# Three small edits in a fused encoder layer: the order of the halves in the w2 tails, the engine of softplus's small steps, and the place of one preparation call

## The chip, the cores and the metric

The kernel runs on one core of one Trainium2 chip, as a single program. The metric is the device time of that program in microseconds: the median of three runs before the change is 1110.12 us (1110.07 to 1110.47). The matrix engine is called PE, the vector engine DVE, the activation engine ACT, GpSimd POOL, and the queue that issues most loads SP.

## The reference, cut to what matters

One layer of a streaming encoder on 512 tokens of width 1024, all in float32:

```python
f = swiglu(rms_norm(h, ffn1_pre_g), w1, w3, w2)       # (silu(u @ w1) * (u @ w3)) @ w2, hidden width 2816
h = h + 0.5 * rms_norm(f, ffn1_post_g)
u = rms_norm(h, mix_pre_g)
q, k, v, xr, xg = split(u @ w_in)
...                                                    # rg_lru uses softplus(-lambda), 1024 values
h = h + rms_norm(merged @ w_o, mix_post_g)
f = swiglu(rms_norm(h, ffn2_pre_g), w1, w3, w2)
y = h + 0.5 * rms_norm(f, ffn2_post_g)
```

The part between is a gated linear recurrence and a windowed attention. Of it only `softplus(-lambda)` matters here: it is computed once for 1024 channels, laid out as 128 partitions by 8 columns, and its results `chalf` and `cneg` are read by the recurrence first at 395.8 us, some 85 us after they are written.

## The kernel before

**Numbers in pairs.** Every float32 operand of a product is split into a high part `hi` (ACT copies it to the matrix engine's rounded float32) and a low part `lo` (DVE subtracts `hi` from the operand). A product is three matmuls: hi times hi, lo times hi, hi times lo. So each weight tile of 128x1024 costs one ACT copy of about 1.05 us and one DVE subtraction of about 1.14 us.

**Order.** The order of instructions on each engine is the order in which the program calls them; every engine runs its own list in that order and waits for what it needs. There is no planner. Buffers in SBUF come from 42 slots of one size, handed out in rotation.

**FFN, up.** `Pairs` (from line 689) computes two columns of blocks of `w1` or `w3` at a time by a seven-product block scheme, with sums and differences of blocks. FFN 1 runs 18 such jobs. While a job's products run on PE, `prep` prepares the next job's operands. In the last job the calls `ahead` and `tail` (both mean `half.prep(half.ready + 1)`) prepare the operands of the first units of the following stage instead.

**FFN, down.** `w2` is handled in two parts. `Halves.run` does rows 4 to 19 of 22 by the same kind of block scheme over halves of 512 columns, in 28 units of 12 matmuls each (lines 616 to 618). `Halves.prep` prepares a unit five units ahead: an ACT copy and a DVE subtraction of the weights, the same for the activations, and one or two DVE sums of blocks (lines 548 and 551). Hooks at given units start other work; one of them, at unit 25 (`SOFTPLUS_AT`), is `softplus`.

The other six rows of `w2` (`TAIL`) follow in `tok_gemm`: for each of the four token tiles t (128 tokens each), PE does 18 matmuls for columns 0 to 511 (n = 0) and 18 for columns 512 to 1023 (n = 1), lines 242 to 244. For t = 0 and 1 both column halves have a part of the block result in SBUF that has to be added (`hc`, from `Halves.part`). For t = 2 and 3 only n = 1 has such a part; n = 0 is complete in PSUM.

**The norm behind the tail.** `post_norm` (line 284) takes a tile's two halves: DVE adds the SBUF parts (line 294), ACT squares and sums each half (line 298), DVE multiplies by the gain `gpost` (line 299, `fg`), a reciprocal root follows (lines 256 to 264), and DVE adds the result to `h` (line 310). In FFN 1 `norms` (line 314) goes on with the next norm (gain `gpre`, `mix_pre_g`) and gives `hg` (lines 325, 333, 334), which PE transposes (line 343, `tr`) after the next tile's matmuls. In FFN 2 the result goes to the output.

The two gains are broadcast to all partitions by DMAs that POOL issues (`bcast`, line 281), called right after the last `w2` row is split; POOL then scales `gpre` (line 410). POOL's earlier work there is DMAs with accumulation (lines 588, 594, 602). While the tail runs, DVE also splits the first four tiles of `xr` (line 179), the first weights of the mixing stage.

`softplus` (line 1121) is two ACT steps and 29 DVE steps on 128x8 or smaller tiles: a chain of a reciprocal and a polynomial (lines 1126 to 1136), the two results, and five copies of biases times 0.5 (lines 1139 and 1143).

Of the kernel before, what the change touches and what calls it, by code (L numbers as in the profile page):

```python
# [12 lines left out]
AF = mybir.ActivationFunctionType  # L13
ALU = mybir.AluOpType
# [3 lines left out]
D = 1024  # L18
# [3 lines left out]
NT = SEQ // P  # L22
# [4 lines left out]
EPS = 1e-6  # L27
# [4 lines left out]
V_CW, V_CB, V_BA, V_BX, V_LAM, V_BG, V_G1, V_SINK, V_N = 0, 32, 40, 48, 56, 64, 80, 88, 104  # L32
# [19 lines left out]
def hybrid_layer(ctx: ExitStack, tc: tile.TileContext, a: dict, out: bass.AP):  # L52
    nc = tc.nc
    act, dve, pool, pe, sp = nc.scalar, nc.vector, nc.gpsimd, nc.tensor, nc.sync
# [38 lines left out]
    h = {}  # L93
# [142 lines left out]
    def mm_tok(acc, x, t, w, first, last, ns=(0, 1), skip=False):  # L236

        wh, wl = w
        c = slice(t * P, (t + 1) * P)
        for n in ns:  # L240
            s = slice(n * 512, (n + 1) * 512)
            pe.matmul(acc[n], x[:, 0, c], wh[:, s], start=first, stop=False, skip_group_check=skip)  # L242
            pe.matmul(acc[n], x[:, 0, c], wl[:, s], start=False, stop=False, skip_group_check=skip)  # L243
            pe.matmul(acc[n], x[:, 1, c], wh[:, s], start=False, stop=last, skip_group_check=skip)  # L244
# [3 lines left out]
    NEWT = -0.5 * D**0.5  # L248
# [32 lines left out]
        pool.dma_start(out=t, in_=bass.AP(tensor=src.tensor, offset=src.offset, ap=[[0, P], [1, D]]))  # L281
        return t

    def post_norm(acc, t, gpost, scale, dst, after=None, last=False, eps=D * EPS, mid=None, part=None):

        ss = small(2, "ss")
        fg = slot([P, D], name="fg")
        junk = slot([P, D], name="junk")
        cs = [slice(n * 512, (n + 1) * 512) for n in range(2)]
        if part:  # L290
            acc = list(acc)
            for n, o in enumerate(part):
                if o is not None:
                    dve.tensor_tensor(out=o, in0=acc[n], in1=o, op=ALU.add)
                    acc[n] = o
        rs = Rstd2()
        for n, c in enumerate(cs):
            act.activation(junk[:, c], acc[n], AF.Square, accum_out=ss[:, n : n + 1])
            dve.scalar_tensor_tensor(out=fg[:, c], in0=acc[n], scalar=scale, in1=gpost[:, c], op0=ALU.mult, op1=ALU.mult)
            if n:  # L300
                rs.root(ss)
            else:
                rs.first(ss, eps)
        r = rs.value()
        if mid:
            mid()
        if last:
            cs = [slice(0, 512), slice(512, 768), slice(768, D)]
        for n, c in enumerate(cs):
            dve.scalar_tensor_tensor(out=dst[:, c], in0=fg[:, c], scalar=r, in1=h[t][:, c], op0=ALU.mult, op1=ALU.add)  # L310
            if after:
                after(n, c)

    def norms(acc, t, gpost, scale, gpre, spill, eps, mid=None, part=None):

        hg = slot([P, D], name="hg")
        junk = slot([P, D], name="junk")
        ss = small(2, "ss")
        rs = Rstd2()

        def half(n, c):
            act.activation(junk[:, c], h[t][:, c], AF.Square, accum_out=ss[:, n : n + 1])
            if n:
                rs.first(ss)
                dve.tensor_tensor(out=hg[:, c], in0=h[t][:, c], in1=gpre[:, c], op=ALU.mult)

        post_norm(acc, t, gpost, scale * NEWT, h[t], half, eps=eps, mid=mid, part=part)
# [5 lines left out]
        dve.scalar_tensor_tensor(out=hg[:, :512], in0=ht[:, :512], scalar=r, in1=gpre[:, :512], op0=ALU.mult, op1=ALU.mult)  # L333
        act.activation(hg[:, 512:], hg[:, 512:], AF.Copy, scale=r)
        return hg
# [30 lines left out]
    def tok_gemm(nm, xs, n, R, gpost_name, scale, gpre_name, first, x_to=None, xf=None, spill=False, then=None, eps=None, pre=None):  # L366
# [36 lines left out]
        tail = list(pre.hid.seq) if pre else list(range(F, n))  # L403
# [3 lines left out]
        gpost = bcast(gpost_name)  # L407
        gpre = bcast(gpre_name) if gpre_name else None
        if gpre_name:
            pool.tensor_scalar(out=gpre, in0=gpre, scalar1=NEWT, scalar2=None, op0=ALU.mult)  # L410
        us, trs = {}, {}
        ep = lambda t: D * EPS if eps is None else eps[:, t : t + 1]
        split_to(st["get"] + len(first))
        dma_to(st["split"] + 2)
        for t in range(NT):
            for ns in ((0,), (1,)):
                for k in tail:
                    new = k == tail[0] and (t > 1 and ns == (1,) if pre else k == 0)
                    mm_tok(accs(t), xs[k], t, w[k], new, k == tail[-1], ns, bool(pre))
            if not gpre_name:  # L420
                o = slot([P, D], name="o")

# [3 lines left out]
                post_norm(acc[t], t, gpost, scale * NEWT, o, store, t == NT - 1, part=pre and pre.part(t))  # L426
# [8 lines left out]
            us[t] = norms(acc[t], t, gpost, scale, gpre, spill, ep(t), part=pre and pre.part(t))  # L435
            if t == 1:
                transpose_out(trs[t - 1], t - 1, xf)
        if not gpre_name:
# [2 lines left out]
        t = NT - 1  # L441
# [16 lines left out]
        us[t] = norms(acc[t], t, gpost, scale, gpre, spill, ep(t), between, pre and pre.part(t))  # L458
# [230 lines left out]
    class Pairs:  # L689
# [65 lines left out]
        def run(self, tail, hooks={}):  # L755
# [3 lines left out]
            last = silu = lambda: None  # L759
            for n, (nm, f) in enumerate(self.jobs):  # L760
# [23 lines left out]
                if n == len(self.jobs) - 1:  # L784
                    silu()
                    silu = lambda: None
                    tail()
                self.prep(n + 1, 2)

                def c11():  # L790
                    mm_s(W["a12"], X["b21"], bc)
                    del W["a11"], W["a12"]
                    dve.tensor_tensor(out=c[:, 0, :256], in0=bc, in1=q1, op=ALU.add)
# [11 lines left out]
                dve.tensor_tensor(out=c[:, 1, 256:], in0=v, in1=q5, op=ALU.add)  # L805
                if n == len(self.jobs) - 1:
                    tail()
                    c11()
                if not first:
                    c1 = self.c1[f]  # L810
# [310 lines left out]
    def softplus():  # L1121
        lam = vec[:, V_LAM : V_LAM + KT]
        z = [small(KT, "z", 5) for _ in range(5)]
        act.activation(z[0], lam, AF.Abs)
        act.activation(z[1], z[0], AF.Exp, scale=-1.0)
        dve.tensor_scalar(out=z[2], in0=z[1], scalar1=2.0, scalar2=None, op0=ALU.add)
        dve.reciprocal(z[2], z[2])
# [6 lines left out]
        dve.tensor_tensor(out=z[3], in0=z[3], in1=z[1], op=ALU.mult)  # L1134
        dve.tensor_scalar(out=z[4], in0=lam, scalar1=-1.0, scalar2=0.0, op0=ALU.mult, op1=ALU.max)
        dve.scalar_tensor_tensor(out=z[3], in0=z[3], scalar=2.0, in1=z[4], op0=ALU.mult, op1=ALU.add)
        dve.tensor_scalar(out=chalf, in0=z[3], scalar1=2.0, scalar2=None, op0=ALU.mult)
        dve.tensor_scalar(out=cneg, in0=z[3], scalar1=-4.0, scalar2=None, op0=ALU.mult)
# [96 lines left out]
    half = None  # L1235
# [527 lines left out]
```

## Time and profile before

| | |
|---|---|
| median of three runs | 1110.12 us |
| profiled execution, its own time | 1110.68 us |
| span of its instructions | 1108.9 us |
| PE busy | 1098.4 us, 99% of the span |
| DVE busy | 912.5 us, 82% |
| ACT busy | 668.9 us, 60% |
| POOL busy | 389.9 us, 35% |
| w2 block units of FFN 1 | 232.5 to 310 us |
| w2 tail of FFN 1 with its norms | 310 to 353 us |
| last matmul of the kernel | issued at 1100.92 us |

PE is counted busy while a matmul is under way, so its 99% says that it is hardly ever without one, and that what is left to win are the short places where a matmul starts late. The other engines work beside it; their shares are averages over stages in which each of them is at some time the one that PE waits for. The profiled execution is 0.56 us above the median.

### The profile page before, as it was taken

The page shows a single profiled execution, that of the slowest core. Times are in us where ns is not written, and L with a number is a line of the kernel's source. Part 1 is how long each engine was busy: PE and PEld are TensorE (multiplying, and loading weights), DVE is VectorE, ACT ScalarE, POOL GpSimd, SP SyncE. Part 2 cuts the span into 40 slices and gives each one's busy share as a digit, 9 for nine tenths or more (in the row PEclk, how much of TensorE's full clock was granted, in tenths as well). Part 3 has the DMA queues.
Part 4 walks back from the last instruction along what each step waited for, and adds up shares of the span by engine and source line. Part 5 has one row for each costly group of instructions (what it writes and reads, how often), then busy time and mean ns, then how long its engine had stood idle before and what let it go on. Part 6 is the DMA issues. An engine that isn't in the chain of part 4 may idle for free.

```text
span 1108.9 us, 17987 instructions
## 1 busy us (share of the span) xinstructions
PE 1098.4 (99%) x6850; PEld 989.6 (89%) x6850; DVE 912.5 (82%) x1337; ACT 668.9 (60%) x1175; POOL 389.9 (35%) x308
## 2 busy tenths in 40 slices
PE   9999999999999999999999999999999999999997
PEld 8899999987879878899888888889999999998885
DVE  5988999999997978887778867767789898689954
ACT  7755555576857678656655654356455555567821
POOL 0143533202212413242656663010976665502100
PEclk9999999999999999999999999999999999999999
DMA  9325663467944642156132435442332323476832
GB/s 338 120 87 140 136 136 115 148 197 159 256 173 186 141 127 79 40 179 239 58 95 77 131 117 223 150 159 95 115 109 83 114 82 110 137 229 148 191 113 76
DMA packets 52662, 155.41 MB, mean 140 GB/s; under 512 B 5456, under 2 KB 7376, under 8 KB 52576
## 3 DMA queue, kind: packets, MB, share of 16 engines
q1 hardware_dynamic: 42256, 129.57, 34.0%
q0 software_dynamic: 10032, 24.16, 11.1%
q8 instruction: 54, 0.88, 0.3%
q10 hardware_dynamic: 288, 0.52, 0.2%
q14 instruction: 32, 0.26, 0.1%
HBM read 138.52 MB, written 13.62 MB: 137 GB/s over the span
## 4 chain that ended last, share of the span: by engine, by line
PE 86%; DVE 10%; DMA 2%; issue 1%; ACT 0%; POOL 0%; DVEq 0%; SPq 0%; POOLq 0%; ACTq 0%
PE c L683 12%; PE c L684 12%; PE c L685 12%; PE f L224 9%; PE f L225 9%; PE f L226 9%; DVE wlo L596 2%; PE acc L243 2%; PE acc L244 2%; PE acc L242 2%; DVE uT L214 1%; DVE raw_w2a L548 1%; PE hw L243 1%; PE hw L244 1%; PE hw L242 1%
## 5 line engine op out<-in xcount | busy, mean ns | idle before, releaser
L684 PE MATMUL c<-uT,wlo 128*128 128x256 f32 x516 | 146.1, 283 | 0.0
L685 PE MATMUL c<-uT,whi 128*128 128x256 f32 x516 | 146.1, 283 | 0.0
L683 PE MATMUL c<-uT,whi 128*128 128x256 f32 x516 | 146.1, 283 | 0.0
L683 PE MATMUL c<-Xh,whi 128*128 128x256 f32 x504 | 142.8, 283 | 0.0
L684 PE MATMUL c<-Xh,wlo 128*128 128x256 f32 x504 | 142.7, 283 | 0.0
L224 PE MATMUL f<-uT,whi 128*128 128x512 f32 (+1 forms) x368 | 136.5, 371 | 0.0
L225 PE MATMUL f<-uT,wlo 128*128 128x512 f32 (+1 forms) x368 | 134.9, 367 | 0.0
L226 PE MATMUL f<-uT,whi 128*128 128x512 f32 (+1 forms) x368 | 134.8, 366 | 0.0
L685 PE MATMUL c<-Xl,whi 128*128 128x256 f32 x456 | 129.1, 283 | 0.0
L214 DVE TENSOR_TENSOR wlo<-S,whi 128x1024 fp32r<-128x1024 f32 x86 | 118.7, 1380 | 8.1 <-POOL OL L1557 4.5
L213 ACT ACTIVATE whi<-S 128x1024 fp32r<-128x1024 f32 x86 | 88.5, 1054 | 31.4 <-DVE S L732 29.7
L684 PEld LDWEIGHTS c<-uT,wlo 128*128 128x128 f32 x516 | 99.1, 192 | 0.2
L683 PEld LDWEIGHTS c<-uT,whi 128*128 128x128 f32 x516 | 99.1, 192 | 0.2
L685 PEld LDWEIGHTS c<-uT,whi 128*128 128x128 f32 x516 | 99.1, 192 | 0.0
L683 PEld LDWEIGHTS c<-Xh,whi 128*128 128x128 f32 x504 | 96.8, 192 | 0.3 <-issue 0.3
L684 PEld LDWEIGHTS c<-Xh,wlo 128*128 128x128 f32 x504 | 96.8, 192 | 0.0
L685 PEld LDWEIGHTS c<-Xl,whi 128*128 128x128 f32 x456 | 87.6, 192 | 0.0
L224 PEld LDWEIGHTS f<-uT,whi 128*128 128x128 f32 x368 | 69.4, 189 | 12.5 <-issue 1.7
L226 PEld LDWEIGHTS f<-uT,whi 128*128 128x128 f32 x368 | 69.4, 188 | 11.4
L225 PEld LDWEIGHTS f<-uT,wlo 128*128 128x128 f32 x368 | 69.5, 189 | 10.8
L1505 POOL TENSOR_SCALAR P<-P,d 128x256 f32<-128x256 f32 (+1 forms) x64 | 62.0, 984 | 45.0 <-DVE d L1503 27.9
L616 PE MATMUL hw<-wlo,uT 128*128 128x512 f32 x192 | 75.2, 392 | 0.4 <-DMA wlo<-in_w2b_dram 0.3
(434 smaller groups left out, 3189.7 us busy)
## 6 DMA issues: line engine op xcount, KB each, us to landing
raw_w2a<-in_w2a_dram SPq DMA_DIRECT2D x22, 512.0 KB, 4.5
raw_w1b<-in_w1b_dram SPq DMA_DIRECT2D x22, 512.0 KB, 4.3
raw_w3b<-in_w3b_dram SPq DMA_DIRECT2D x22, 512.0 KB, 4.3
raw_w2b<-in_w2b_dram SPq DMA_DIRECT2D x22, 512.0 KB, 4.6
raw_w3a<-in_w3a_dram SPq DMA_DIRECT2D x21, 512.0 KB, 4.4
raw_w1a<-in_w1a_dram SPq DMA_DIRECT2D x20, 512.0 KB, 4.5
raw_wg<-in_wg_dram SPq DMA_DIRECT2D x16, 512.0 KB, 4.0
h<-in_x_dram SPq DMA_DIRECT2D x8, 512.0 KB, 6.9
```

The lines of the kernel that those rows point to most:

```text
L213: act.activation(hi, src, AF.Copy)
L214: dve.tensor_tensor(out=lo, in0=src, in1=f32(hi), op=ALU.subtract)
L224: pe.matmul(ps[:, c0:c1], wh[:, s], h_, start=k == 0 and c0 == 0, stop=False, skip_group_check=True)
L225: pe.matmul(ps[:, c0:c1], wl[:, s], h_, start=False, stop=False, skip_group_check=True)
L226: pe.matmul(ps[:, c0:c1], wh[:, s], l_, start=False, stop=k == KT - 1, skip_group_check=True)
L242: pe.matmul(acc[n], x[:, 0, c], wh[:, s], start=first, stop=False, skip_group_check=skip)
L243: pe.matmul(acc[n], x[:, 0, c], wl[:, s], start=False, stop=False, skip_group_check=skip)
L616: pe.matmul(ps, xs[:, 0, j, c], lo[:, j, :], start=False, stop=False, skip_group_check=True)
L683: pe.matmul(ps, wh[:, s], xh, start=first, stop=False, skip_group_check=True)
L684: pe.matmul(ps, wl[:, s], xh, start=False, stop=False, skip_group_check=True)
L685: pe.matmul(ps, wh[:, s], xl, start=False, stop=k == 3, skip_group_check=True)
L1505: pool.tensor_scalar(out=pt[:, x, b0:256], in0=pt[:, x, b0:256], scalar1=d[:, x : x + 1], scalar2=None, op0=ALU.mult)
```

## The change

Three edits.

1. For t = 2 and 3 of both w2 tails PE does n = 1 first and n = 0 second. `post_norm` now goes over the halves in the same order, and does each half whole (add, square, multiply by the gain) before it turns to the other one. For t = 0 and 1 the order of the halves stays 0, 1, but the DVE add of the second half now stands behind the first half's multiplication and its small step of line 256, where before both adds came first.
2. In `softplus`, DVE keeps three steps (add 2, reciprocal, the maximum `z[4]`). The rest, 26 DVE instructions, becomes 28 POOL instructions (two fused steps are written as two each).
3. In the last job of FFN 1's `Pairs`, the first `tail()`, which prepares unit 2 of the block units, is called after the product `s3` and its two additions rather than before the product `s4`. FFN 2's job (`self.R` is None) stays as it was.

```diff
-    def post_norm(acc, t, gpost, scale, dst, after=None, last=False, eps=D * EPS, mid=None, part=None):
+    def post_norm(acc, t, gpost, scale, dst, after=None, last=False, eps=D * EPS, mid=None, part=None, ns=(0, 1)):
...
-        if part:
-            acc = list(acc)
-            for n, o in enumerate(part):
-                if o is not None:
-                    dve.tensor_tensor(out=o, in0=acc[n], in1=o, op=ALU.add)
-                    acc[n] = o
         rs = Rstd2()
-        for n, c in enumerate(cs):
-            act.activation(junk[:, c], acc[n], AF.Square, accum_out=ss[:, n : n + 1])
-            dve.scalar_tensor_tensor(out=fg[:, c], in0=acc[n], scalar=scale, in1=gpost[:, c], op0=ALU.mult, op1=ALU.mult)
-            if n:
+        for j, n in enumerate(ns):
+            c, x, o = cs[n], acc[n], part and part[n]
+            if o is not None:
+                dve.tensor_tensor(out=o, in0=x, in1=o, op=ALU.add)
+                x = o
+            act.activation(junk[:, c], x, AF.Square, accum_out=ss[:, j : j + 1])
+            dve.scalar_tensor_tensor(out=fg[:, c], in0=x, scalar=scale, in1=gpost[:, c], op0=ALU.mult, op1=ALU.mult)
+            if j:
                 rs.root(ss)
             else:
                 rs.first(ss, eps)
...
+        halves = lambda t: (1, 0) if pre and t > 1 else (0, 1)
...
-            for ns in ((0,), (1,)):
+            for n_ in halves(t):
                 for k in tail:
-                    new = k == tail[0] and (t > 1 and ns == (1,) if pre else k == 0)
-                    mm_tok(accs(t), xs[k], t, w[k], new, k == tail[-1], ns, bool(pre))
+                    new = k == tail[0] and (t > 1 and n_ == 1 if pre else k == 0)
+                    mm_tok(accs(t), xs[k], t, w[k], new, k == tail[-1], (n_,), bool(pre))
...
                 if n == len(self.jobs) - 1:
                     silu()
                     silu = lambda: None
-                    tail()
+                    if self.R is None:
+                        tail()
                 self.prep(n + 1, 2)
...
                 if n == len(self.jobs) - 1:
                     tail()
+                    if self.R is not None:
+                        tail()
                     c11()
...
         dve.tensor_scalar(out=z[2], in0=z[1], scalar1=2.0, scalar2=None, op0=ALU.add)
         dve.reciprocal(z[2], z[2])
-        dve.tensor_tensor(out=z[1], in0=z[1], in1=z[2], op=ALU.mult)
-        dve.tensor_tensor(out=z[2], in0=z[1], in1=z[1], op=ALU.mult)
-        dve.tensor_scalar(out=z[3], in0=z[2], scalar1=1.0 / 17, scalar2=1.0 / 15, op0=ALU.mult, op1=ALU.add)
+        dve.tensor_scalar(out=z[4], in0=lam, scalar1=-1.0, scalar2=0.0, op0=ALU.mult, op1=ALU.max)
+        e = pool
+        e.tensor_tensor(out=z[1], in0=z[1], in1=z[2], op=ALU.mult)
+        e.tensor_tensor(out=z[2], in0=z[1], in1=z[1], op=ALU.mult)
+        e.tensor_scalar(out=z[3], in0=z[2], scalar1=1.0 / 17, scalar2=None, op0=ALU.mult)
+        e.tensor_scalar(out=z[3], in0=z[3], scalar1=1.0 / 15, scalar2=None, op0=ALU.add)
         for c in (13, 11, 9, 7, 5, 3, 1):
-            dve.tensor_tensor(out=z[3], in0=z[3], in1=z[2], op=ALU.mult)
-            dve.tensor_scalar(out=z[3], in0=z[3], scalar1=1.0 / c, scalar2=None, op0=ALU.add)
+            e.tensor_tensor(out=z[3], in0=z[3], in1=z[2], op=ALU.mult)
+            e.tensor_scalar(out=z[3], in0=z[3], scalar1=1.0 / c, scalar2=None, op0=ALU.add)
...
-        dve.tensor_scalar(out=bhalf, in0=vec[:, V_BA : V_BG + 16], scalar1=0.5, scalar2=None, op0=ALU.mult)
+        e.tensor_scalar(out=bhalf, in0=vec[:, V_BA : V_BG + 16], scalar1=0.5, scalar2=None, op0=ALU.mult)
...
-                dve.tensor_scalar(
+                e.tensor_scalar(
                     out=bxh[r0 : r0 + 64, par, :], in0=vec[64 * par : 64 * par + 64, V_BX : V_BX + KT],
```

More of the change, by code (lines that the diff above doesn't have):

```diff
@@ L312, in post_norm, with norms @@
                 after(n, c)
-    def norms(acc, t, gpost, scale, gpre, spill, eps, mid=None, part=None):
+    def norms(acc, t, gpost, scale, gpre, spill, eps, mid=None, part=None, ns=(0, 1)):
         hg = slot([P, D], name="hg")
@@ L325, in half @@
                 dve.tensor_tensor(out=hg[:, c], in0=h[t][:, c], in1=gpre[:, c], op=ALU.mult)
-        post_norm(acc, t, gpost, scale * NEWT, h[t], half, eps=eps, mid=mid, part=part)
+        post_norm(acc, t, gpost, scale * NEWT, h[t], half, eps=eps, mid=mid, part=part, ns=ns)
         ht = h[t]
@@ L424, in store @@
                     sp.dma_start(out=out[t * P : (t + 1) * P, c], in_=o[:, c])
-                post_norm(acc[t], t, gpost, scale * NEWT, o, store, t == NT - 1, part=pre and pre.part(t))
+                post_norm(acc[t], t, gpost, scale * NEWT, o, store, t == NT - 1, part=pre and pre.part(t), ns=halves(t))
                 continue
@@ L434, in tok_gemm @@
                 transpose_out(trs[t - 1], t - 1)
-            us[t] = norms(acc[t], t, gpost, scale, gpre, spill, ep(t), part=pre and pre.part(t))
+            us[t] = norms(acc[t], t, gpost, scale, gpre, spill, ep(t), part=pre and pre.part(t), ns=halves(t))
             if t == 1:
@@ L457, in tok_gemm @@
         mm_feat(bs[0], ws[0], 0, 256, ks=range(3, KT))
-        us[t] = norms(acc[t], t, gpost, scale, gpre, spill, ep(t), between, pre and pre.part(t))
+        us[t] = norms(acc[t], t, gpost, scale, gpre, spill, ep(t), between, pre and pre.part(t), halves(t))
         transpose_out(trs[t - 1], t - 1, parts=(1,))
@@ L1127, in softplus @@
         dve.reciprocal(z[2], z[2])
-        dve.tensor_tensor(out=z[1], in0=z[1], in1=z[2], op=ALU.mult)
-        dve.tensor_tensor(out=z[2], in0=z[1], in1=z[1], op=ALU.mult)
-        dve.tensor_scalar(out=z[3], in0=z[2], scalar1=1.0 / 17, scalar2=1.0 / 15, op0=ALU.mult, op1=ALU.add)
-        for c in (13, 11, 9, 7, 5, 3, 1):
-            dve.tensor_tensor(out=z[3], in0=z[3], in1=z[2], op=ALU.mult)
-            dve.tensor_scalar(out=z[3], in0=z[3], scalar1=1.0 / c, scalar2=None, op0=ALU.add)
-        dve.tensor_tensor(out=z[3], in0=z[3], in1=z[1], op=ALU.mult)
@@ L1135, in softplus @@
[L1135 to L1138, printed above, removed]
-        dve.tensor_scalar(out=bhalf, in0=vec[:, V_BA : V_BG + 16], scalar1=0.5, scalar2=None, op0=ALU.mult)
+        dve.tensor_scalar(out=z[4], in0=lam, scalar1=-1.0, scalar2=0.0, op0=ALU.mult, op1=ALU.max)
@@ new lines, in softplus @@
+        e.tensor_tensor(out=z[3], in0=z[3], in1=z[1], op=ALU.mult)
+        e.tensor_scalar(out=z[3], in0=z[3], scalar1=2.0, scalar2=None, op0=ALU.mult)
+        e.tensor_tensor(out=z[3], in0=z[3], in1=z[4], op=ALU.add)
+        e.tensor_scalar(out=chalf, in0=z[3], scalar1=2.0, scalar2=None, op0=ALU.mult)
+        e.tensor_scalar(out=cneg, in0=z[3], scalar1=-4.0, scalar2=None, op0=ALU.mult)
+        e.tensor_scalar(out=bhalf, in0=vec[:, V_BA : V_BG + 16], scalar1=0.5, scalar2=None, op0=ALU.mult)
```

## The prediction

> **What bounds the kernel now.** First the page and the waits of PE, then the order of time on DVE, POOL and PE around the places that the diff touches.
>
> ```profile
> span 1108.9 us, 17987 instructions
> PE hw L243 <- DVE wlo L179: 0.7, 1, 0.7
> PE c L683 <- ACT ct L804: 0.3, 1, 0.3
> ```
>
> The waits' columns are the total in us, how often, and the longest. Of a span of 1108.9 us, the sums to win on PE are these two waits, and what lies behind the last matmul. So the change can win at most about 2 us; what it can lose is not bounded by that. The first wait is at 314 us, in the w2 tail of FFN 1. The order of time on DVE there (start, duration):
>
> ```profile
> 306.63 0.16 DVE L1126 TENSOR_SCALAR z<-z 128x8 f32<-128x8 f32 x1
> 306.82 0.20 DVE L1127 RECIPROCAL z<-z 128x8 f32<-128x8 f32 x1
> 312.84 0.69 DVE L214 TENSOR_TENSOR hT<-kept,hT 128x512 fp32r<-128x512 f32 x1
> 313.45 1.22 DVE L179 TENSOR_TENSOR wlo<-raw_w2a,whi 128x1024 fp32r<-128x1024 f32 x1
> 314.59 4.62 DVE L179 TENSOR_TENSOR wlo<-raw_xr,whi 128x1024 fp32r<-128x1024 f32 x4
> 319.13 1.28 DVE L294 TENSOR_TENSOR hc<-hw,hc 128x512 f32<-128x512 f32 x2
> 320.33 0.68 DVE L299 SCALAR_TENSOR_TENSOR fg<-hc,bc_ffn_post_g 128x512 f32<-128x512 f32 x1
> 320.93 0.20 DVE L256 TENSOR_SCALAR b<-ss,veps 128x1 f32<-128x1 f32 x1
> 325.01 0.69 DVE L325 TENSOR_TENSOR hg<-h,bc_mix_pre_g 128x512 f32<-128x512 f32 x1
> 326.50 0.75 DVE L333 SCALAR_TENSOR_TENSOR hg<-h,r,bc_mix_pre_g 128x512 f32<-128x512 f32 x1
> 333.70 0.75 DVE L333 SCALAR_TENSOR_TENSOR hg<-h,r,bc_mix_pre_g 128x512 f32<-128x512 f32 x1
> ```
>
> And on PE:
>
> ```profile
> 314.73 0.50 PE L243 MATMUL hw<-wlo,hT 128*128 128x512 f32 x1 [0.67 <-DVE wlo L179]
> 327.60 0.60 PE L343 MATMUL tr<-ident,hg 128*128 128x128 f32 x4
> 336.65 0.60 PE L343 MATMUL tr<-ident,hg 128*128 128x128 f32 x4
> ```
>
> Softplus holds DVE from 306.63 to 312.84, and the last `w2` split (313.45) stands behind it; PE waits 0.67 us for that split. The row to keep in mind is 327.60: PE transposes tile 0's `hg`, which DVE finished at 326.50 + 0.75 = 327.25. That is 0.35 us before PE wanted it. Whatever delays tile 0's norm by more than that delays PE.
>
> **Edit 2: what POOL's queue carries.** After the change softplus stands on POOL ahead of these three:
>
> ```profile
> 299.85 0.59 POOL L281 DMA_DIRECT2D bc_ffn_post_g<-in_ffn_post_g_dram  x1 [11.95 <-PE hw L617]
> 304.06 0.55 POOL L281 DMA_DIRECT2D bc_mix_pre_g<-in_mix_pre_g_dram  x1 [3.62 <-DVE wlo L596]
> 311.38 2.79 POOL L410 TENSOR_SCALAR bc_mix_pre_g<-bc_mix_pre_g 128x1024 f32<-128x1024 f32 x1 [6.77 <-DMA bc_mix_pre_g<-in_mix_pre_g_dram]
> ```
>
> These are the gains' broadcasts. `gpost` is issued at 299.85, before softplus begins, and line 299 reads it at 320.33. POOL's first small step needs DVE's reciprocal (306.82 + 0.20), so POOL starts softplus at about 307.1 and issues `gpost` only when its 28 steps are done, at a time T. The trace shows no POOL step of 8 columns. The nearest rows (duration minimum/median/maximum in ns, and one group with its idle time):
>
> ```profile
> L1505 POOL TENSOR_SCALAR P<-P,d x64: 592/922/1804, 527.8 to 654.8; 128x256 f32<-128x256 f32 x48, 128x128 f32<-128x128 f32 x16
> L1557 POOL TENSOR_TENSOR OL<-o,OH x16: 729/735/1474, 559.8 to 677.3; 128x256 fp32r<-128x256 f32 x16
> L1362 POOL TENSOR_TENSOR xf<-xf,xf x4: 2412/3262/3272, 355.9 to 365.1; 128x1024 f32<-128x1024 f32 x4
> L737 POOL TENSOR_TENSOR S<-S,raw_w1b 128x512 f32<-128x512 f32 x10 | 16.7, 1668 | 0.8
> ```
>
> Two inputs: 729 ns at 256 columns and 2412 at 1024 give 2.19 ns a column and 168 ns fixed, so 0.19 us at 8 columns. One input: 592 at 128 (the minimum) and 922 at 256 give 2.58 ns a column and 262 fixed, 0.28 us at 8; line 410's 2.79 us at 1024 leaves only about 0.15 fixed, 0.17 at 8; I take 0.23 between them. Steps that read the step before start 0.08 us later (line 737: 0.8 us over 10). So 11 x 0.19 + 17 x 0.23 + 22 x 0.08 = 7.8 us, or 0.28 us a step, if POOL is left alone: T = 314.9. From above, no step costs more than the 592 ns of the smallest one measured.
>
> POOL is not left alone. In another stage, POOL's rows and DVE's of the same moments, the last one the same line on DVE without POOL:
>
> ```profile
> 124.19 2.25 POOL L736 TENSOR_TENSOR S<-raw_w3a 128x512 f32<-128x512 f32 x1 [5.21 <-PE c L685]
> 126.53 2.16 POOL L737 TENSOR_TENSOR S<-S,raw_w3a 128x512 f32<-128x512 f32 x1
> ...
> 124.07 1.22 DVE L214 TENSOR_TENSOR wlo<-raw_w1a,whi 128x1024 fp32r<-128x1024 f32 x1 [1.17 <-ACT whi L213]
> 125.21 2.32 DVE L823 TENSOR_TENSOR cc<-cc,Rb 128x1024 f32<-128x1024 f32 x1
> ...
> 226.91 1.22 DVE L823 TENSOR_TENSOR cc<-cc,Rb 128x1024 f32<-128x1024 f32 x1
> ```
>
> POOL's step of 124.19 ends at 126.44, some 1.15 us after DVE's subtraction of 124.07 ended at 125.29; DVE's next takes 2.32 instead of 1.22 and ends at 127.53; POOL's next ends at 128.69, again 1.16 us after that. The two take turns, one instruction each, when DVE reads two SBUF tensors. Between 307.2 and about 314.4 DVE has six such instructions: the last `hT` and `w2` splits, then four splits of `xr`. Taking turns lets POOL through once for each, so with the first step and one in a gap some 8 steps are done by 314.4. Then DVE stands at line 299 and waits for `gpost` itself, and the other 20 steps run freely: 20 x 0.26 (the last five depend on nothing before them) = 5.1 us. T = 319.5.
>
> [...]
>
> How long the broadcast then takes, for the five that line 281 issues, and how full the DMA engines are (in a row of windows the last two figures are the DMA share and GB/s):
>
> ```profile
> DMA to landing us min/median/max: 4.0/5.9/7.2
> ...
> 305.00:310.00 5.00, 5.00 (x23) 4.14 (x23) 4.45 (x19) 1.58 (x2) 0.00 (x0) 1.00 1.01 404
> 320.00:325.00 5.00, 5.00 (x24) 4.14 (x23) 3.83 (x10) 3.58 (x9) 0.00 (x0) 1.00 0.01 3
> ```
>
> At 320 to 325 us the DMA engines were idle before the change, so I take 4.0, with 7.2 for the range. `gpost` lands at 323.5. The two broadcasts no longer share the full DMA engines at 305 us, so `xr` lands earlier; that shifts DVE's six turns, not their number.
>
> [...]
>
> From there: line 299 for the first half (0.6 from start to start), line 256 (0.13), and now the second half's add behind them (0.65) with a start-up of 0.1: that add ends at 325.0. Before it ended at 319.13 + 1.28 = 320.41 and `hg` at 327.25, 6.84 us later. So `hg` is ready at 331.8 and PE's transposes start at 331.9, not 327.60: **4.3 us late**. `gpre` follows `gpost` by 0.6 us and is scaled by T + 0.6 + 4.0 + 2.8 = 326.9; line 325 wants it 2.24 us before `hg` is done, at 329.6, so it is covered by 2.7 us.
>
> The 26 steps taken from DVE bring the last `w2` split forward and end PE's 0.67 us wait. PE then only waits longer at the transposes: worth nothing here, 0.7 us if `gpost` were in time. Tile 1 is next: its norm took from 327.25 to 334.45, 7.2 us, and its second add now stands behind line 256, which waits for ACT's first sum; that adds up to 0.9. PE asks for it 336.65 - 327.60 = 9.05 us after tile 0's transposes, so it stays covered, with 0.9 us left.
>
> **Edit 1.** At the end of the kernel:
>
> ```profile
> 1101.35 0.69 DVE L294 TENSOR_TENSOR hc<-acc,hc 128x512 f32<-128x512 f32 x1 [4.01 <-PE acc L244]
> ...
> 1097.27 0.60 ACT L298 ACTIVATE junk<-hw 128x512 f32<-128x512 f32 x1 [2.30 <-PE hw L244]
> 1102.07 0.63 ACT L298 ACTIVATE junk<-hc 128x512 f32<-128x512 f32 x1 [4.12 <-DVE hc L294]
> ```
>
> The last half was the one with the add: DVE at 1101.35, then ACT's square at 1102.07. Now the last half is complete in PSUM, ACT squares it at 1101.35, in 0.60 rather than 0.63 us: **0.75 us less**, all on the path, since reciprocal root, line 310 and the store follow one another. It cannot be more than the add's 0.72 + 0.03; it would be less if ACT's start from PSUM came later than DVE's. In FFN 1 tiles 2 and 3 gain the same where PE does not wait: nothing.
>
> **Edit 3.** PE, ACT and DVE around the second wait and where PE next meets DVE:
>
> ```profile
> 229.13 1.04 ACT L591 ACTIVATE whi<-raw_w2a 128x1024 fp32r<-128x1024 f32 x1
> 230.59 0.36 ACT L804 ACTIVATE ct<-c 128x256 f32<-128x256 f32 x1
> ...
> 248.95 0.68 DVE L214 TENSOR_TENSOR uT<-hEO,uT 128x512 fp32r<-128x512 f32 x1
> ...
> 249.69 0.49 PE L617 MATMUL hw<-whi,uT 128*128 128x512 f32 x1
> ```
>
> ACT drains `s3` (line 804) at 230.59 behind unit 2's copies; called later, the copies no longer stand ahead of it, and the wait of 0.3 (0.5 with the slow start behind it) goes. But at 249.69 PE starts on an operand that DVE finishes at 249.63. DVE does the same instructions in between, without idle time, in a slightly other order, so PE gets there earlier and waits longer: **0**, with 0.5 gained or 0.3 lost (a unit's operand late) for the range. The moved call also carries one load on SP; nothing else is issued on SP between its two places.
>
> **Sum.** 4.3 - 0.75 + 0 = +3.5 us. Against the profiled execution 1110.68 + 3.5 = 1114.2; it stands 0.56 above the median, so in terms of the median of 1110.12 it is 1113.6 us.
>
> **The rivals.**
> 1. Not slower: POOL's small steps slip in between DVE's. If T is 315.1 or less, `gpost` lands by 319.1, `hg` is ready by 327.4 and PE does not wait; then the 0.7 and the 0.75 are both won, 1108.7 us. The whole change breaks even at T = 315.9. For it: 7.8 us of POOL work alone gives 314.9. Against it: the turns at 124 to 129 us. Chance 0.20.
> 2. Small steps on POOL cost as much as the smallest measured one, 592 ns. Then 20 of them take 11.8 instead of 5.1 us: 6.7 us more, 1120.3 us. For it: that row is the only direct one. Against it: durations fall in line with columns in both kinds. Chance 0.10.
> 3. Edit 3's gain is kept, since DVE has slack that the records hide: 0.5 less, 1113.1. Against it: 249.63 and 249.69. Chance 0.06.
>
> **How the numbers follow.** My forecast has 0.64: T from 317.5 to 322 and landings of 4.0 to 7.2 give 1111.6 to 1118. Outside about 0.2% (2.2 us), which a measurement of this kernel can tell from no change, faster than 1107.9 would need more than all three gains together: 0.04. Within it lie rival 1 and the lowest part of the forecast: 0.26. Slower: 0.70. The range of 1109.0 to 1118.5 leaves out half of rival 1 and rival 2, some 0.2.
>
> **What would show it.** Right: `gpost` issued by POOL near 319 us, not 300; DVE idle ahead of line 299 until it lands; PE idle for some 4 us ahead of the first `tr`; small POOL steps of 0.2 to 0.3 us, stretched to over 1 us beside DVE's splits; the last square on ACT 0.43 us behind the last matmul; the wait at 231 us gone and that at 249 us longer. Wrong: POOL's steps undisturbed and `gpost` issued by 315, or a landing so early that PE never waits.

## The result, and the profile after

| | before | after |
|---|---|---|
| median of 6 runs, us | 1110.39 (1110.07 to 1112.00) | 1118.65 (1118.25 to 1121.51) |
| ratio of after to before | | 1.0076, 95% interval 1.0064 to 1.0089 |
| the profiled execution, its span | 1110.68, 1108.9 | 1121.51, 1119.7 |

The change costs 8.3 us; the forecast was 3.5, and 1118.65 lies just above the range that ended at 1118.5. The profiled execution of after is the longest of its six, 2.9 us above their median, so not every microsecond of its trace is there in the median. What is not repeated is named below.

The page of after begins with its span. Its longest waits of PE (total in us, how often, the longest):

```profile
span 1119.7 us, 17983 instructions
...
PE tr L341 <- DVE hg L331: 6.7, 2, 5.8
PE hw L615 <- DMA wlo<-in_w2b_dram: 1.5, 2, 0.9
...
PE f L224 <- DVE o L1557: 0.5, 1, 0.5
```

A new wait leads the list: PE's transposes of `hg` (line 341 is line 343 of before), 6.7 us in two places, 5.76 and 0.97. Before, this pair of lines was not in the list.

The order of time on POOL in the tail of FFN 1 (start, duration; in brackets, the idle time before and what ended it):

```profile
307.32 0.54 POOL L1132 TENSOR_TENSOR z<-z,z 128x8 f32<-128x8 f32 x1 [19.27 <-DVE z L1130]
307.94 1.06 POOL L1133 TENSOR_TENSOR z<-z 128x8 f32<-128x8 f32 x1
...
309.43 0.25 POOL L1135 TENSOR_SCALAR z<-z 128x8 f32<-128x8 f32 x1
309.76 0.20 POOL L1137 TENSOR_TENSOR z<-z,z 128x8 f32<-128x8 f32 x1
310.05 1.12 POOL L1138 TENSOR_SCALAR z<-z 128x8 f32<-128x8 f32 x1
311.25 1.23 POOL L1137 TENSOR_TENSOR z<-z,z 128x8 f32<-128x8 f32 x1
...
314.95 1.10 POOL L1137 TENSOR_TENSOR z<-z,z 128x8 f32<-128x8 f32 x1
316.14 0.23 POOL L1138 TENSOR_SCALAR z<-z 128x8 f32<-128x8 f32 x1
...
320.62 0.65 POOL L281 DMA_DIRECT2D bc_ffn_post_g<-in_ffn_post_g_dram  x1
...
326.24 2.77 POOL L408 TENSOR_SCALAR bc_mix_pre_g<-bc_mix_pre_g 128x1024 f32<-128x1024 f32 x1 [4.40 <-DMA bc_mix_pre_g<-in_mix_pre_g_dram]
```

Read here the two kinds of step. Left alone, an 8-column step takes 0.20 to 0.25 us and the next begins 0.3 us after it began; beside DVE's splits it takes 1.06 to 1.23 us. And the broadcast of `gpost` stands at 320.62, where it was at 299.85.

DVE in the same time:

```profile
309.86 2.56 DVE L179 TENSOR_TENSOR wlo<-raw_xr,whi 128x1024 fp32r<-128x1024 f32 x2 [0.91 <-ACT whi L178]
313.51 2.48 DVE L179 TENSOR_TENSOR wlo<-raw_xr,whi 128x1024 fp32r<-128x1024 f32 x2 [1.09 <-ACT whi L178]
...
324.95 0.69 DVE L297 SCALAR_TENSOR_TENSOR fg<-hc,bc_ffn_post_g 128x512 f32<-128x512 f32 x1 [8.36 <-DMA bc_ffn_post_g<-in_ffn_post_g_dram]
...
325.68 0.68 DVE L294 TENSOR_TENSOR hc<-hw,hc 128x512 f32<-128x512 f32 x1
...
332.42 0.75 DVE L331 SCALAR_TENSOR_TENSOR hg<-h,r,bc_mix_pre_g 128x512 f32<-128x512 f32 x1
```

DVE stands 8.36 us before line 297, until `gpost` has landed, and goes on at 324.95, 4.3 us after its issue. `hg` of tile 0 is done at 333.17. On PE that reads:

```profile
333.22 1.97 PE L341 MATMUL tr<-ident,hg 128*128 128x128 f32 x8 [5.76 <-DVE hg L331]
335.84 0.63 PE L244 MATMUL acc<-whi,hT 128*128 128x512 f32 x1
336.27 0.63 PE L242 MATMUL acc<-whi,hT 128*128 128x512 f32 x1
...
361.96 1.09 PE L341 MATMUL tr<-ident,hg 128*128 128x128 f32 x8 [0.97 <-DVE hg L331]
```

The first row is the wait that was forecast, 5.76 us long. The next two show what was not: behind the wait, matmuls of 512 columns start 0.43 us apart and take 0.63 instead of 0.39 us. The windows say why (columns: stretch, length, busy time and count of PE, PEld, DVE, ACT and POOL, granted clock, DMA share, GB/s):

```profile
330.00:333.00 3.00, 0.00 (x0) 0.00 (x0) 2.69 (x8) 2.27 (x6) 0.00 (x0) 0.77 0.43 175
333.00:336.00 3.00, 2.78 (x11) 2.59 (x12) 2.87 (x6) 1.46 (x5) 0.00 (x0) 0.50 0.00 0
336.00:339.00 3.00, 3.00 (x10) 2.34 (x9) 2.62 (x8) 1.59 (x6) 0.00 (x0) 0.59 0.00 0
339.00:342.00 3.00, 3.00 (x15) 2.49 (x14) 2.33 (x7) 2.21 (x6) 0.00 (x0) 1.00 0.43 175
```

The granted clock falls while PE waits: a mean of 0.77 over 330 to 333 is full clock until about 331.6 and half behind it, and PE's last matmul ended at 327.46, 4.2 us earlier. It is still 0.50 when PE comes back, and full again only at about 338.4, after 5.2 us of work. PE looks busy there (3.00 of 3.00 us), but only 10 matmuls go through in 3 us where 15 do at full clock.

To see where the time went, compare starts of the same PE instructions in both traces. The last column is what the step adds. The stage began 0.7 us later than before; most of that arose at 291 to 298 us, ahead of it, and the long wait takes it up.

| PE instruction | before | after | later by | added |
|---|---|---|---|---|
| first wait for a `w2` split, tail of FFN 1 | 314.73 | 314.61 | -0.12 | -0.8 since the stage began |
| transposes of tile 0's `hg` | 327.60 | 333.22 | 5.62 | 5.74 |
| a matmul once the clock is full again | 330.30 | 338.40 | 8.10 | 2.48 |
| last transposes of the tail | 352.67 | 361.96 | 9.29 | 1.19 |
| a matmul of the next stage | 551.81 | 561.82 | 10.0 | 0.7 |
| `w2` of FFN 2 | 1055 | 1066.4 | 11.4 | 1.4 |
| end of the span | 1108.9 | 1119.7 | 10.8 | -0.5 |

The tail of FFN 1 and the end of the kernel make 9.29 - 0.54 = 8.75 us, close to the 8.3 of the medians. The 0.7 and the 1.4 further down stand where after waits for a DMA-fed `wlo` and for line 1557; these waits come and go between the profiles of the kernels below, and their sum of 2.1 is most of the 2.9 by which this execution lies above its median. That they are not the change's is argued from that, not shown.

### The profile page after: what moved, and what is told of

Same layout as the page of the kernel before. It is cut to its first block, busy times and chain, and to the rows that moved or that the text cites. A ratio compares the mean times of both kernels' runs of the same rounds, so it can differ in the third digit from the quotient of the medians.

```text
span 1119.7 us, 17983 instructions
## 1 busy us (share of the span) xinstructions
PE 1101.4 (98%) x6850; PEld 990.6 (88%) x6850; DVE 911.9 (81%) x1311; ACT 669.5 (60%) x1175; POOL 400.9 (36%) x336
## 4 chain that ended last, share of the span: by engine, by line
PE 83%; DVE 8%; DMA 2%; ACT 2%; issue 2%; POOL 2%; DVEq 0%; SPq 0%; POOLq 0%; ACTq 0%
PE c L682 13%; PE c L684 13%; PE c L683 13%; PE f L224 8%; PE f L225 8%; PE f L226 8%; PE hw L616 2%; PE hw L615 2%; PE hw L614 2%; PE acc L242 2%; PE acc L243 2%; PE acc L244 2%; DVE wlo L595 2%; DMA wlo<-in_w2b_dram 1%; PE pt L1526 1%
## 5 line engine op out<-in xcount | busy, mean ns | idle before, releaser
L226 PEld LDWEIGHTS f<-uT,whi 128*128 128x128 f32 x368 | 69.4, 189 | 11.4
```

The lines of the kernel that those rows point to most:

```text
L226: pe.matmul(ps[:, c0:c1], wh[:, s], l_, start=False, stop=k == KT - 1, skip_group_check=True)
```

## The experiments

### One edit at a time

Edit 1 alone, the order of the halves. Shown against after: edits 3 and 2 are taken back.

```diff
-                    if self.R is None:
-                        tail()
+                    tail()
...
-                    if self.R is not None:
-                        tail()
...
+        dve.tensor_tensor(out=z[1], in0=z[1], in1=z[2], op=ALU.mult)
...
-        e = pool
-        e.tensor_tensor(out=z[1], in0=z[1], in1=z[2], op=ALU.mult)
...
```

> Edit 1 alone: the order of the halves in the w2 tails, softplus on DVE and the preparation call as before. Theory A (the gains queued behind softplus make the loss): the end is 0.5 us shorter (in the changed kernel 7.06 us from the last matmul's end to the last instruction against 7.60), and there is no long wait at the first transposes. Reading the order on DVE, the norm of tile 0 gets its second add some 0.9 us later, because it now stands behind line 256 that waits for ACT's first sum, so PE waits 0.5 to 0.9 us at the first transposes, and tile 3's squares stand one behind the other on ACT after the add, which costs up to 0.8 at the last transposes: 1110.4 + 1.0, between 1109.6 and 1111.6. Theory B (the new order of the halves is what delays the norms, and GpSimd only adds to it): at least half of the 8.3 us, 1114.5 or more.

Measured 1112.51 against 1110.69: 1.0016 (1.0007 to 1.0025). PE's longest wait:

```profile
PE tr L341 <- DVE hg L331: 1.7, 2, 1.2
```

So edit 1 is not free in FFN 1: it makes PE wait at the first transposes of the tail and, longer, at the last. Its profiled execution is the slowest of its runs (1114.72): it is 2.3 us late already ahead of every line of edit 1, where POOL issues `gpost` (302.12, in the trace of before 299.85). So its size is better read from the median: about 1.8 us worse, although the end of the kernel is 0.54 us shorter in this trace too.

Edit 2 alone, softplus's steps on POOL:

```diff
-        dve.tensor_tensor(out=z[1], in0=z[1], in1=z[2], op=ALU.mult)
...
+        dve.tensor_scalar(out=z[4], in0=lam, scalar1=-1.0, scalar2=0.0, op0=ALU.mult, op1=ALU.max)
+        e = pool
+        e.tensor_tensor(out=z[1], in0=z[1], in1=z[2], op=ALU.mult)
...
```

> Edit 2 alone: softplus's small steps on GpSimd, the halves and the preparation call as before. Theory A: the broadcast of gpost is issued at 320 to 321 us again and lands at 325. But with both adds and both squares ahead of line 299, the root no longer waits behind the gain, so the first transposes start near 331 us instead of 333: 3.5 us later than before the change, an idle time of about 4 us, and then 0 to 2.4 us more if the matrix engine's clock drops behind it. 1114 to 1116.5. Theory B: the wait at the first transposes stays under 2 us and the time under 1112.

Measured 1117.06 against 1110.69: 1.0053 (1.0039 to 1.0067). Its issue of `gpost` on POOL and its transposes on PE:

```profile
320.47 0.64 POOL L281 DMA_DIRECT2D bc_ffn_post_g<-in_ffn_post_g_dram  x1
```

```profile
331.98 0.47 PE L343 MATMUL tr<-ident,hg 128*128 128x128 f32 x1 [5.16 <-DVE hg L333]
```

The transposes are 331.98 - 327.60 = 4.4 us late, the clock is 0.50 behind them and costs 2.1 more; 6.5 us by the trace, 6.4 by the medians. At the last transposes PE does not wait. So the large part of the change, with its clock, is edit 2's.

Edit 3 alone, the unit called later:

```diff
-                    tail()
+                    if self.R is None:
+                        tail()
...
                     tail()
+                    if self.R is not None:
+                        tail()
```

> Edit 3 alone: one preparation call of FFN 1 later. Theory A (DVE sets the pace up to 253 us): the wait of 0.5 us at 231 us goes and the waits at 246 to 253 us grow by as much, no difference, 1110.4 within 0.3. Rival: the 0.5 us is kept, 1109.9.

Measured 1110.98 against 1110.69: 1.0000 (0.9991 to 1.0009). Edit 3 is worth nothing.

Edits 1 and 3 together, softplus left on DVE. Shown against after: edit 2 is taken back.

```diff
+        dve.tensor_tensor(out=z[1], in0=z[1], in1=z[2], op=ALU.mult)
...
-        e = pool
-        e.tensor_tensor(out=z[1], in0=z[1], in1=z[2], op=ALU.mult)
...
```

> The changed kernel with softplus put back on DVE, that is edits 1 and 3. Theory A: as edit 1 alone, 1110.4 + 1.0, between 1109.6 and 1111.6, and gpost issued near 300 us. Theory B: 1114.5 or more.

Measured 1112.58 against 1110.69: 1.0013 (1.0004 to 1.0022), with one wait at the transposes:

```profile
PE tr L341 <- DVE hg L331: 1.4, 1, 1.4
```

It is the one at the last transposes. In this profile a DMA wait of 1.6 us at 291 to 299 us came earlier and left DVE more time, so the first one does not show; the cost of edit 1 is confirmed all the same. Ratio by ratio, the three edits alone make 0.16 + 0.53 + 0.00 = 0.69%, together 0.76%.

### Is it the queue, or POOL's steps?

After, with softplus called behind the gains' broadcasts and the scaling of `gpre`; the steps stay on POOL and only their place in its queue changes:

```diff
-    half.hooks[SOFTPLUS_AT].append(softplus)
+    half.softplus = softplus
...
             pool.tensor_scalar(out=gpre, in0=gpre, scalar1=NEWT, scalar2=None, op0=ALU.mult)
+        if pre and gpre_name:
+            pre.softplus()
```

> The changed kernel with one thing moved: softplus is called behind the two broadcasts and the scaling of gpre, so the same 28 GpSimd steps stand behind the gains in GpSimd's queue. Theory A (the gains' place in the queue makes the loss of edit 2): gpost is issued near 300 us, the 4 to 6 us wait at the first transposes is gone and with it the slow clock; what is left is edit 1's 1.7 us, less up to 0.7 for the wait at 314 us: 1110.4 to 1112.5. Rival C (the steps harm by taking turns with DVE, wherever they stand): the turns now fall into the norms of tiles 0 and 1, and the time stays at 1114 or more.

Measured 1110.04 against 1110.35: 0.9996 (0.9987 to 1.0005). POOL issues `gpost` early again, and PE starts the transposes without a wait:

```profile
299.87 0.59 POOL L281 DMA_DIRECT2D bc_ffn_post_g<-in_ffn_post_g_dram  x1 [12.20 <-PE hw L618]
```

```profile
326.61 1.03 PE L341 MATMUL tr<-ident,hg 128*128 128x128 f32 x8
```

All of edit 2's loss came from where the steps stood in POOL's queue: 1118.65 against 1110.04. (That is more than the 6.4 us of edit 2 alone. Beside edit 1 a late `gpost` delays the transposes by 5.62 instead of 4.4 us, and with the steps behind the gains the wait at 314 us is won, some 1.0 us.) The steps themselves still take turns with DVE (1.06 us at 314.77) and cost PE nothing there. What is left is a wait of 1.0 us at the last transposes, as in the kernels with edit 1.

Twelve more small steps ahead of the broadcasts, multiplying by 2 and by a half in turn, which leaves the value as it was:

```diff
+        for _ in range(6):
+            e.tensor_scalar(out=z[3], in0=z[3], scalar1=2.0, scalar2=None, op0=ALU.mult)
+            e.tensor_scalar(out=z[3], in0=z[3], scalar1=0.5, scalar2=None, op0=ALU.mult)
         e.tensor_tensor(out=z[3], in0=z[3], in1=z[1], op=ALU.mult)
```

> The changed kernel with 12 more small GpSimd steps (times 2, times 0.5, in turn, which leaves the value as it was) inside softplus, ahead of the gains. At 0.30 to 0.31 us from start to start they take 3.7 us. Theory A (GpSimd's queue is the path): gpost is issued 3.7 us later, at 324.3, the first transposes start 3.7 us later, and the whole takes 3.7 us more, 1122.3, between 1121.5 and 1123. Theory B: less than 1 us more.

Measured 1122.05 against 1110.35: 1.0103 (1.0089 to 1.0116), 3.4 us above after. Its broadcast and its transposes:

```profile
324.59 0.65 POOL L281 DMA_DIRECT2D bc_ffn_post_g<-in_ffn_post_g_dram  x1
```

```profile
337.30 1.12 PE L341 MATMUL tr<-ident,hg 128*128 128x128 f32 x4 [9.68 <-DVE hg L331]
```

The twelve steps move the issue by 3.97 us, 0.33 each, and the transposes by 4.08: the path runs from POOL's queue to PE, one for one.

### What the clock costs

After, with 26 matmuls issued while PE waits, ahead of the tail's first transposes, into the bank that these then overwrite; so this kernel computes something extra whose result is thrown away:

```diff
-    def transpose_mm(hg):
+    def transpose_mm(hg, wf=None):
...
             ps = bank("tr")
+            if wf is not None and half == 0:
+                for _ in range(26):
+                    pe.matmul(ps, wf[:, :P], wf[:, :512], start=True, stop=True)
...
-                trs[t - 1] = transpose_mm(us[t - 1])
+                trs[t - 1] = transpose_mm(us[t - 1], w[tail[0]][0] if t == 1 and pre and gpre_name else None)
```

> The changed kernel with 26 extra matmuls (their result is overwritten, they compute nothing of use) between tile 1's tail and the first transposes, in the bank that the transposes then write: about 5.9 us of work in the place of the 5.8 us of idle time. Theory A (the idle time also lowers the matrix engine's clock, granted 0.50 at 333 to 336 us, which costs 2.4 us): the transposes start at the same time or up to 0.3 later, the matmuls behind them take 227 ns at once instead of 427, 1116.4, between 1115.8 and 1117.2. Rival D (the matmuls behind the transposes are slow for another reason, such as operands that come late): 1118.6 or more, and the 427 ns stay.

Measured 1117.05 against 1110.35: 1.0057 (1.0043 to 1.0071), 1.6 us below after by the medians and 2.1 by the ratios, although PE does more. Its window and the matmuls behind the transposes:

```profile
333.00:336.00 3.00, 3.00 (x19) 2.62 (x18) 2.74 (x6) 1.73 (x5) 0.00 (x0) 1.00 0.00 0
```

```profile
332.94 1.03 PE L344 MATMUL tr<-ident,hg 128*128 128x128 f32 x8
334.28 0.40 PE L244 MATMUL acc<-whi,hT 128*128 128x512 f32 x1
334.51 0.39 PE L242 MATMUL acc<-whi,hT 128*128 128x512 f32 x1
```

The transposes stay late (332.94), but the clock is 1.00, eight transposes take 1.03 instead of 1.97 us, and the matmuls follow 0.23 us apart. The slow stretch is a cost of PE's idle time, apart from the wait itself. Of the 2.5 us that it costs in the trace of after, 1.6 to 2.1 are seen in the times.

### Which parts are worth keeping

Edit 2 behind the gains and edit 3 as before, the halves swapped only in FFN 2, and in the tiles that are not swapped both adds first, as in the kernel before:

```diff
-        halves = lambda t: (1, 0) if pre and t > 1 else (0, 1)
+        halves = lambda t: (1, 0) if pre and t > 1 and not gpre_name else (0, 1)
...
+        if ns == (0, 1):
+            add(0), add(1)
         for j, n in enumerate(ns):
+            if ns != (0, 1):
+                add(n)
```

> Softplus's GpSimd steps behind the gains, edit 3 as it is, and the swapped order of the halves in FFN 2 alone; tiles with two parts in SBUF get both adds first, as before the change. Theory A: nothing of the losses is left, 0.5 us won at the end and up to 0.7 at 314 us: 1109.2 to 1110, at or below the kernel before. Rival C: the turns between DVE and GpSimd in the norms cost 1 us or more, 1111.5 or more.

Measured 1108.98 against 1110.35: 0.9984 (0.9976 to 0.9993). It is faster than both kernels. The whole list of PE's waits:

```profile
PE w L1003 <- POOL warm L1000: 1.1, 1, 1.1
PE f L1053 <- ACT uT L1046: 0.3, 1, 0.3
```

No transposes are in it. By the starts, 0.54 us is gained at the tail's first matmuls, 1.05 by `w2` of FFN 2, 1.16 by the last matmul, and the end is 0.53 shorter: 1.7 in this trace, 1.4 by the medians. About 0.3 of it is a wait of before for a DMA-fed `wlo` in FFN 2, which does not recur here.

The same with the halves of tiles 2 and 3 swapped in FFN 1 as well:

```diff
-        halves = lambda t: (1, 0) if pre and t > 1 and not gpre_name else (0, 1)
+        halves = lambda t: (1, 0) if pre and t > 1 else (0, 1)
```

> As the end-only kernel (1108.98 us), but with the swapped halves in FFN 1's tiles 2 and 3 as well; tiles 0 and 1 keep both adds first. Theory E (in FFN 1 the swap puts both squares behind the add on ACT, 0.54 us later at the root for tile 2 and again for tile 3, and tile 3's transposes were only just in time): a wait of about 1 us at the last transposes, 1110.0. Rival F (the adds of tiles 0 and 1, one behind the other's small step, are what makes the last transposes late): no wait there, 1109.0.

Measured 1111.08 (1109.66 to 1112.68 over 11 runs) against 1110.34: 1.0002 (0.9993 to 1.0011). One wait is back, at the last transposes:

```profile
PE tr L350 <- DVE hg L340: 1.0, 1, 1.0
```

So the swap in FFN 1 costs about the 1.0 us of that wait; its medians differ by 2.1, but it spreads over 3 us and the size is not settled. Since tiles 0 and 1 have both adds first here and the wait is back all the same, their order is not its cause. Why it costs, one sees at tile 3's squares. First the kernel with softplus behind the gains, where FFN 1 is swapped, then the kernel that swaps only in FFN 2 (lines 294 and 296 are the add, 296 and 305 the square, 259 the root):

```profile
345.42 0.68 DVE L294 TENSOR_TENSOR hc<-acc,hc 128x512 f32<-128x512 f32 x1
...
346.13 0.63 ACT L296 ACTIVATE junk<-hc 128x512 f32<-128x512 f32 x1 [0.66 <-DVE hc L294]
346.76 0.58 ACT L296 ACTIVATE junk<-hw 128x512 f32<-128x512 f32 x1
347.46 0.29 ACT L259 ACTIVATE r<-ss,b 128x1 f32<-128x1 f32 x1
```

```profile
344.92 0.58 ACT L305 ACTIVATE junk<-hw 128x512 f32<-128x512 f32 x1
...
345.19 0.69 DVE L296 TENSOR_TENSOR hc<-acc,hc 128x512 f32<-128x512 f32 x1
...
345.91 0.63 ACT L305 ACTIVATE junk<-hc 128x512 f32<-128x512 f32 x1 [0.33 <-DVE hc L296]
346.69 0.29 ACT L259 ACTIVATE r<-ss,b 128x1 f32<-128x1 f32 x1
```

Unswapped, ACT squares the half that needs no add while DVE adds. Swapped, ACT waits for the add and has both squares behind it: from the add's start to the root 2.04 us instead of 1.50. At the end of the kernel PE's last half sets the pace and the swap helps; here both halves lie in PSUM by the time DVE comes to the tile (in the swapped kernel PE's last matmul of it ends at 344.87 and the add starts at 345.42), and the swap lengthens the chain by 0.54 us for tile 3, and as much for tile 2.

Last, softplus behind the gains but on DVE, else like the kernel that swaps only in FFN 2, and shown against it:

```diff
+        dve.tensor_tensor(out=z[1], in0=z[1], in1=z[2], op=ALU.mult)
...
-        e = pool
-        e.tensor_tensor(out=z[1], in0=z[1], in1=z[2], op=ALU.mult)
...
```

> As the end-only kernel, but with softplus's steps on DVE as before the change, called behind the gains, so they stand behind the last w2 split on DVE too. Theory G (moving softplus behind the last split is worth the same on either engine, and DVE then has the 5 us ahead of tile 0's norm again): the wait at 314 us is gone, PE arrives 0.7 us earlier at the first transposes, hg is ready when it was before, so 0.4 us is lost there: 1109.4. Rival H (GpSimd is what wins): 1109.7 or more. Rival I (DVE has room): 1109.0.

Measured 1110.67 against 1110.34: 1.0001 (0.9992 to 1.0010), with a wait at the first transposes:

```profile
PE tr L350 <- DVE hg L340: 1.4, 1, 1.4
```

On DVE PE waits for tile 0's norm again; on POOL, at the same place in the program, it does not. So GpSimd is the better engine for softplus by some 1.7 us (1108.98 against 1110.67), as long as nothing urgent stands behind it in POOL's queue.

## Why the prediction was right and wrong

**Sign and mechanism: right.** The broadcast of `gpost` behind softplus on POOL's queue, DVE idle ahead of it, PE idle at the transposes: each is in the trace, moving the steps behind the gains takes the loss away, and lengthening them adds to it one for one.

**Edit 2, small steps: right.** Forecast 0.19 and 0.23 us with 0.08 between; measured 0.20 and 0.23 to 0.25, starting 0.30 us apart. Rival 2 (0.59 us each) is out. The turns with DVE were right too: five steps of 1.06 to 1.23 us, against rival 1, in which small steps slip through.

**T: 320.62, forecast 319.5.** More steps were through by 314.4 than expected (11, not 8), but the turns lasted longer: DVE's splits of `xr` stood twice for ACT (0.91 and 1.09 us) and ended at 315.99, not 314.4. From 316.14 the last 15 steps ran freely, 4.4 us. From the issue to the start of line 297 it was 4.3 us, forecast 4.0. (The forecast's 20 x 0.26 is 5.2, not 5.1; that is 0.1 us.)

**From `gpost` to the transposes: right.** The second add ended at 325.68 + 0.68 = 326.36 and `hg` was done at 333.17, 6.81 us later; forecast 6.84. The 5.62 us of delay, forecast 4.3, are so the 1.1 of T and the 0.3 of the landing. `gpre` was scaled by 326.24 + 2.77 = 329.01 and not waited for, and tile 1's transposes did not wait: both as forecast. The 0.67 us of the `w2` split was won (0.8 by the table) and lost in the longer wait, as forecast.

**The missed term: PE's clock, 2.1 to 2.5 us.** The step "PE's transposes start at 331.9, not 327.60: 4.3 us late" took the lateness of the first transposes as the whole cost, as if PE went on at its old pace. It came back at a granted clock of 0.50 (333 to 336 us), and the matmuls there started 427 instead of 227 ns apart until 338.4. The trace of before, on which the sum was made, has no idle time of PE near 4 us in this stage (the longest wait there is 0.67 us), so no row of the stage showed it. But the end of that trace does show the fall, behind the last matmul, which ended at 1101.31:

```profile
1104.00:1106.00 2.00, 0.00 (x0) 0.00 (x0) 1.59 (x4) 0.00 (x0) 0.00 (x0) 0.83 0.15 58
1106.00:1108.00 2.00, 0.00 (x0) 0.00 (x0) 0.00 (x0) 0.00 (x0) 0.00 (x0) 0.50 0.57 204
```

A mean of 0.83 over 1104 to 1106 puts it at about 1105.3, 4.0 us into PE's idle time, less than the forecast wait; what it costs when PE comes back stands in neither row. The trace of after falls to 0.50 as well, 4.2 us into the wait, and is back at 1.00 after 5.2 us of work; with edit 2 alone the fall came 2.8 us into the wait (a mean of 0.79 over 325 to 333 is full clock until about 329.6, and PE's last matmul ended at 326.82). With the 2.1 us that edit 2 alone shows, the forecast would have been as much higher.

**The missed term: edit 1 in FFN 1, 1.2 us in the whole change.** "In FFN 1 tiles 2 and 3 gain the same where PE does not wait: nothing" looked only for a gain. It left out that where both halves are already there, the swap puts both squares behind the add, 0.54 us for each tile, and that `hg` of the last transposes had less slack than that. Alone, edit 1 makes the kernel 1.8 us slower although it wins 0.54 at the end; PE then waits 0.55 us at the first transposes too.

**Edit 1 at the end: 0.54 won, 0.75 forecast.** ACT's and DVE's rows at the end of after:

```profile
1112.71 0.60 ACT L296 ACTIVATE junk<-hw 128x512 f32<-128x512 f32 x1 [2.63 <-PE hw L244]
...
1113.43 0.69 DVE L297 SCALAR_TENSOR_TENSOR fg<-hw,bc_ffn_post_g 128x512 f32<-128x512 f32 x1 [3.16 <-ACT junk L296]
...
1114.91 1.54 DVE L308 SCALAR_TENSOR_TENSOR o<-fg,r,h 128x512 f32<-128x512 f32 x3
```

The last matmul starts at 1112.29, so ACT's square comes 0.42 us behind it, as forecast (0.43). But DVE's line 297 now starts only when that square is over, and from the square's start to line 308 it is 2.20 us where it was 1104.08 - 1102.07 = 2.01. That 0.19 is what the forecast's "all on the path" left out; why line 297 stands behind ACT was not tried. The same trace shows only where it does: at 1109.36 the square and line 297 of the half with the add, which both read from SBUF, start at the same moment, and the half in PSUM is the one where DVE waits.

**Edit 3: right.** The wait at 231 us went (0.52 us) and was given back at 246 to 250. Rival 3 is out.

**The sum by what was measured:** 5.62 + 2.48 + 1.19 - 0.54 = 8.75 us against the forecast's 4.3 - 0.75 = 3.5. Of the 5.2 between them the clock is 2.5, T and the landing 1.3, the swap in FFN 1 1.2 and the end 0.2.

**The bounds.** "T from 317.5 to 322 and landings of 4.0 to 7.2 give 1111.6 to 1118" is short at its upper end: 2.5 us of T and 3.2 of the landing on top of 1113.6 make 1119.3. That range would have held 1118.65, but by luck: the T and the landing that were measured make 1115.0 of the forecast, and the rest is terms that it did not have. Rival 1's 1108.7 was 0.4 too low by its own terms: at T = 314.9 `hg` is ready at 327.2, and PE, rid of its wait at 314 us, asks for it at 326.9.

## What to carry to other kernels

When small work moves to an engine that also issues transfers, count what stands behind it in that engine's queue before counting its own cost: here the same 28 steps cost 8.6 us more ahead of two broadcasts than behind them. When a forecast leaves TensorE idle for several microseconds, add a term for the clock on its return: here 5.16 us of idle time cost 2.1 us more behind it, and 5.76 us cost 2.5. An order of two halves that shortens a tail where TensorE sets the pace lengthens the chain where the vector engine does (here 0.54 us won at the end of the kernel, and 0.54 us longer for each tile in FFN 1); use it only in the former.

## What the hardware showed beyond what was expected

- After 5.16 and 5.76 us without work, PE's granted clock was 0.50 for another 4.5 and 5.2 us of work, which cost 2.1 and 2.5 us; after 9.68 us it was 4.5 us (0.50 over 336 to 339, a mean of 0.54 over 339 to 342). In the kernels with no wait above 1.4 us at the transposes, the mean granted clock of the profiled execution was 0.998 or 0.999, against 0.994 to 0.996 in these three. Throwaway matmuls in the idle time kept it at 1.00 and made the whole 1.6 us faster.
- POOL's 8-column steps are short, 0.20 to 0.25 us, and start 0.30 us apart when each depends on the last; yet in the trace of after the five that met DVE's subtractions of two SBUF tensors took 1.06 to 1.23 us. Several pass in the gaps that DVE leaves while it waits (four short ones from 312.57 to 313.69 in the trace of after, between two splits), so the number through by 314.4 us (11) came from DVE's gaps as well as from its instructions.
- In the trace of after the broadcast of `gpost`, 512 KB, landed 4.2 us after its issue at 320.62, with a DMA share of 0.00 over 318 to 320; in the trace of before, issued at 299.85 beside other traffic (a share of 0.99 over 300 to 303), it took 7.0 us.
